# A planned attention block on one core: eleven seven-product steps instead of nine, their late halves issued behind the next step, and a causal mask added by a matmul

## The chip, the cores and the metric

The kernel runs on one NeuronCore of one Trainium2 chip. The metric is the device time of one execution in microseconds (us), lower is better. A core has a matmul engine (PE, with its weight loads shown as PEld), a vector engine (DVE), an activation engine (ACT), a general engine (POOL), a queue engine (SP) and 16 DMA engines that they share. Each engine works through its own instructions in the order in which they were written; an instruction that needs another engine's result waits on a semaphore, and everything behind it on its engine waits too.

## The reference

The input x is 256 rows of 4096 float32 numbers. With DEPTH = 1 only the attention layer and the two norms are computed, all to float32 accuracy:

```
proj = rms_norm(x, norm_attn) @ w_in        # 4096 x 16384
q, k, v, g = split(proj, 4)                 # 32 heads of 128 each
z = q @ k.T / sqrt(128)                     # strictly causal: s < t
log_fail = where(causal, log_sigmoid(-z), 0)
suffix = reverse_cumsum(log_fail) - log_fail
a = where(causal, exp(log_sigmoid(z) + suffix), 0)
o = a @ v
h = x + (o * silu(g)) @ w_out               # 4096 x 4096
out = rms_norm(h, final_norm)
```

## The kernel before

**Products.** The two large products, x by w_in and o by w_out, are cut into *units* of two pairs of columns and, inside a unit, into 16 *steps* of 256 rows of the weights. In one step a 2 x 2 block of activations meets a 2 x 2 block of weights. Written out plainly, this takes eight block products. A step listed in `SEVEN` uses a Strassen-like scheme of seven block products instead, for which three more sums of weight blocks have to be made. Every block product is done three times on PE (high x high, high x low, low x high), because each float32 number is split into a high part in the matmul's own reduced float32 format and the low rest. One such matmul is 128x512. The results of a unit gather in seven PSUM banks (`acc`); the DVE and ACT combine them at the unit's end (`combine`). Unit 0 of w_in and the first unit of w_out use eight products throughout ("plain"); units 1 to 15 of w_in and two units of w_out are "mixed".

**What a step needs.** SP loads two raw tiles (`raw..._0` and `raw..._1`, 256 KB in each of two DMAs) into a ring of 7 (`RAW_BUFS`). For a step with seven products POOL then adds a further block into the second tile by two accumulating DMAs (`add_block`). ACT casts a raw piece to the high part (`wh`), and DVE subtracts to get the low part (`wl`). A step with eight products has two such pieces of 128x1024. A step with seven has four, called parts 0 to 3: 128x1024, 128x512, 128x1024, 128x1024. Parts 2 and 3, the late half, are cast from sums: the DVE first makes three additions in place in the raw tiles (`sums`, L424), which wait for POOL's accumulation and for the low parts of parts 0 and 1. So a late part goes DVE sum, ACT cast, DVE subtraction, PE. The pieces of 128x1024 live in a ring of 5 pairs (`PAIRS`).

**Attention.** Each w_in unit of the mixed kind yields two heads. A head is turned by PE (`tr`), its scores are computed (`z`), ACT makes Abs, Exp, Ln and a scaling (`f`), DVE makes `f = max(z,0) + f`, and then a minimum with the constant `bound` zeroes what lies on and above the diagonal; a matmul by a triangle of -1 makes the suffix sums, ACT makes the weights `a`, and DVE masks `a` again by a minimum with `bound`; two matmuls give `o`. So DVE has two mask instructions of 128x256 per head.

**The order.** The text is not written in the order of the instructions. `Plan` (L95) keeps a clock of its own: every piece of work has an engine, an assumed cost and a due time (`key`); whenever an engine falls free in that plan, the ready work with the earliest due time is emitted on it. The products stand on PE in the order of the list `parts`; the due times of casts, subtractions and sums follow from it.

Of the kernel before, what the change touches and what calls it, by code (L numbers as in the profile page):

```python
# [19 lines left out]
P = 128  # L20
# [11 lines left out]
NS = KC // KT  # L32
EPS = 1e-6

WARM = 9

SEVEN = (1,3,5,7,8,10,11,13,14)
RAW_BUFS = 7
PAIRS = 5
SINGLES = 2
# [3 lines left out]
HEADS_AHEAD = 3  # L49
HEADS_LATER = 12  # L50
AHEAD, SUMS_AHEAD = 4.0, 3.0
PIPE = 0
BLOCKS_LATER = 2


# [175 lines left out]
def kernel(  # L231
# [10 lines left out]
    nc = Plan(tc)  # L242
# [22 lines left out]
    OUT0 = len(units)  # L265
# [7 lines left out]
    for u, (kind, w, cols) in enumerate(units):  # L273
        for s in range(NS):
            if kind == "single":
                if s % 2 == 0:
                    quads.append(((w, cols[0], s), (w, cols[0], s + 1)))
                b = ((1, 6), (7, 2))[u - LAST + 1]
                which = [plain_part(s % 2, *b)]
            else:  # L280
                quads.append(tuple((w, c, s) for c in cols))
                if kind == "plain":
                    which = [
                        plain_part(0, PLAIN["C11"], PLAIN["C21"]),
                        plain_part(1, PLAIN["C12"], PLAIN["C22"]),
                    ]
                else:
                    which = SEVEN_PARTS if s in (SEVEN) else EIGHT_PARTS
            for i, (k, place, prods) in enumerate(which):
                parts.append(  # L290
                    dict(u=u, s=s, i=i, tile=(len(quads) - 1, k), place=place, prods=prods, quad=len(quads) - 1,
                         seven=which is SEVEN_PARTS, size=place.stop - place.start)
                )

    if PIPE:
        late, turn = [], []
        for k, p in enumerate(parts):
            if p["seven"] and p["i"] > 1 and p["s"] < NS - 1:
                late.append(p)
                continue  # L300
            turn.append(p)
            if late and p["s"] != late[0]["s"] and (p["i"] == 1 if p["seven"] else p["i"] == 0):
                now = [q for q in late if q["s"] < p["s"] or q["u"] < p["u"]]
                turn += now
                late = [q for q in late if q not in now]
        assert not late and len(turn) == len(parts)
        parts = turn
# [43 lines left out]
    def ten(emit, *n):  # L351
        return nc.work("tensor", 90 + sum(tensor_ns(m) for m in n), emit, nc.here - 1e4, wait=400)

    def moved(engine, emit, sizes, key, after=None, hold=False, adds=False):
        issue = 550 if engine == "gpsimd" else 330
        return nc.work(
            engine, issue * len(sizes), emit, key, after=after, hold=hold, moves=[(4 * P * n, adds) for n in sizes]
        )
# [128 lines left out]
    forms = {}  # L487

    def new_forms(i, what):
        n = len(SEVEN_FORMS if i in SEVEN else EIGHT_FORMS)  # L490
# [11 lines left out]
    def sums_of(i, y, what, key):  # L502

        tt = nc.vector.tensor_tensor
        if i not in SEVEN:
# [83 lines left out]
    for _ in range(WARM):  # L589
# [2 lines left out]
    ident = ap.tile([P, P], F32, name="ident")  # L592
    make_identity(tc.nc, ident)

    bound = ap.tile([P, 1, P], F32, name="bound")
    nc.gpsimd.memset(bound, 3e38)
    nc.gpsimd.affine_select(
        out=bound, in_=bound, compare_op=ALU.is_gt, fill=0.0, base=0,
        pattern=[[0, 1], [1, P]], channel_multiplier=-1,
    )  # L600

    tri_f = ap.tile([P, P], F32, tag="qkl", name="tri_f")
# [184 lines left out]


    BW = 3 * P
    masked = bound.broadcast_to([P, 2, P])  # L790

    def diagonal(f):
        return f[:, 0 : 2 * P].rearrange("p (a b) -> p a b", a=2)

    def head(u, i):
        yield nc.take("att", "qkh")
        tr = att.tile([P, 2, S], F32, tag="att", name=f"tr{u}_{i}")
# [21 lines left out]
        yield ten(scores, *FULL_P, *FULL_S)  # L819
        nc.give("qkh")  # L820
        yield nc.take("f")

# [9 lines left out]
        yield dve(  # L832
            lambda: nc.vector.scalar_tensor_tensor(out=f, in0=z, scalar=0.0, in1=f, op0=ALU.max, op1=ALU.add), BW
        )
        yield dve(lambda: nc.vector.tensor_tensor(out=diagonal(f), in0=diagonal(f), in1=masked, op=ALU.min), 2 * P)
        yield nc.take("qkh", "qkl")
        fh = ap.tile([P, BW], F32R, tag="qkh", name=f"fh{u}_{i}")
        fl = ap.tile([P, BW], F32R, tag="qkl", name=f"fl{u}_{i}")
# [21 lines left out]
        yield act(weights_of, (BW, BW))  # L860
        nc.give("att")
        nc.start(gated_with(u, i))
        yield dve(lambda: nc.vector.tensor_tensor(out=diagonal(a), in0=diagonal(a), in1=masked, op=ALU.min), 2 * P)
        yield nc.until(("gated", u, i))
        o = st["both", u, i][:, 1, :]
        v = lambda t: st["gv", u][:, t, CW + i * P : CW + (i + 1) * P]
# [60 lines left out]
    def blocks_of_heads(s):  # L927
# [13 lines left out]
        if s in SEVEN:  # L941
# [217 lines left out]
    def products():  # L1159
        for g, (n, k) in enumerate(order):  # L1160
# [3 lines left out]
            if u < 1:  # L1164
                what = "s"
            elif u < OUT0:
                what = "n"
            elif u == OUT0:
                what = "o"
            else:  # L1170
                what = "r" if u > LAST - 2 and s in SEVEN else "p"
# [25 lines left out]
    for s in SEVEN:  # L1197
        nc.start(again(s))
    nc.start(single_h())
    nc.run()  # L1200
# [38 lines left out]
```

## Time and profile before

| | us |
|---|---|
| device time, median of 3 runs | 1755.45 (1755.28 to 1757.99) |
| profiled execution, first to last instruction (span) | 1754.0 |
| PE busy | 1736.9 (99%) |
| DVE busy | 1560.4 (89%) |
| ACT busy | 1166.4 (67%) |
| POOL busy | 295.7 (17%) |

The profile gives no time of the profiled execution beyond its span, so the span stands for it: 1.45 us under the median of the runs. Busy time counts an instruction to the end that the profile tells. On DVE the next instruction starts a little before that end when nothing holds it, so that an instruction of 1.22 us can have its successor 1.13 us after its start. The w_in units lie from the start to about 1400 us, the w_out units behind them.

### The profile page before, as it was taken

Reading aid. Unit: us, or ns where it says so; the run is one execution under the profiler, and the core shown is the slowest. Engines: PE = TensorE matmul, PEld = TensorE weight load, DVE = VectorE, ACT = ScalarE, POOL = GpSimd, SP = SyncE. Lnnn points to the kernel's source line nnn. Section 1 sums busy time; section 2 is a strip of 40 time slices with the busy share of each in tenths; the row PEclk is TensorE's granted clock in tenths of the full one; section 3 lists DMA queues with packets and bytes.
Section 4 is the critical chain, followed back from the end, with each engine's and each line's share of the span. In section 5 each row is a group of like instructions: output and inputs, shape, how many; then the busy total and the mean of one; then the engine's idle time right before and its main releaser. Section 6 shows DMA issues by size and latency. Waiting matters only on the chain.

```text
span 1754.0 us, 24699 instructions
## 1 busy us (share of the span) xinstructions
PE 1736.9 (99%) x7806; PEld 1427.1 (81%) x7806; DVE 1560.4 (89%) x1971; ACT 1166.4 (67%) x1594; POOL 295.7 (17%) x364
## 2 busy tenths in 40 slices
PE   8999999999999999999999999999999999999997
PEld 6888888888888888888888888888888888888885
DVE  7889999999999999999999999999999997899963
ACT  7975767676767676767676767676767675666543
POOL 0012121111111121211111111111112111111100
PEclk9999999999999999999999999999999999999998
DMA  9968777777777878787878787878786877889874
GB/s 340 316 192 224 230 218 229 223 223 226 222 228 217 239 210 239 208 245 210 240 208 245 208 239 206 242 202 245 200 246 200 262 244 239 229 245 271 257 236 156
DMA packets 242867, 405.86 MB, mean 231 GB/s; under 512 B 27520, under 2 KB 67968, under 8 KB 242736
## 3 DMA queue, kind: packets, MB, share of 16 engines
q1 hardware_dynamic: 193968, 352.15, 60.8%
q0 software_dynamic: 47184, 49.76, 17.3%
q10 hardware_dynamic: 1584, 2.38, 0.4%
q8 instruction: 61, 1.00, 0.2%
q14 instruction: 70, 0.57, 0.1%
HBM read 396.05 MB, written 8.13 MB: 230 GB/s over the span
## 4 chain that ended last, share of the span: by engine, by line
PE 92%; DVE 3%; issue 2%; DMA 2%; ACT 1%; SPq 0%; ACTq 0%; DVEq 0%
PE acc L115 87%; PE z L115 2%; DVE wl L115 2%; PE o L115 2%; DMA raw<-in_w_in_dram 1%; PE tr L115 1%; ACT wh L115 1%; DVE raw L115 0%; ACT h L115 0%; SPq L115 0%; DMA xres<-in_x_dram 0%; DMA raw<-in_w_out_dram 0%; ACTq L115 0%; DVE gv_sb L115 0%; DVE h L115 0%
## 5 line engine op out<-in xcount | busy, mean ns | idle before, releaser
L115 ACT CAST wh<-raw 128x1024 fp32r<-128x1024 f32 (+1 forms) x948 | 886.1, 976 | 476.1 <-issue 173.3
L115 DVE TENSOR_TENSOR wl<-raw,wh 128x1024 fp32r<-128x1024 f32 (+1 forms) x948 | 1032.1, 1131 | 125.3 <-ACT wh L115 118.6
L115 PE MATMUL acc<-wh,sh 128*128 128x512 f32 x1913 | 762.6, 399 | 2.4 <-DVE sh L115 2.1
L115 PE MATMUL acc<-wh,sl 128*128 128x512 f32 x1913 | 746.2, 390 | 0.0
L115 PE MATMUL acc<-wl,sh 128*128 128x512 f32 x1913 | 744.9, 389 | 0.8 <-DVE wl L115 0.8
L115 PEld LDWEIGHTS acc<-wh,sh 128*128 128x128 f32 x1913 | 359.4, 188 | 77.3 <-DVE gv_sb L115 3.9
L115 PEld LDWEIGHTS acc<-wh,sl 128*128 128x128 f32 x1913 | 359.1, 188 | 76.9 <-DVE sl L115 0.8
L115 PEld LDWEIGHTS acc<-wl,sh 128*128 128x128 f32 x1913 | 359.7, 188 | 71.5 <-DVE wl L115 1.5
L115 POOL DMA_DIRECT2D raw<-in_w_in_dram x270 | 236.1, 987 | 1075.7 <-DMA raw<-in_w_in_dram 403.1
L115 DVE TENSOR_TENSOR raw<-raw,raw 128x512 f32<-128x512 f32 x306 | 210.3, 687 | 5.1
L115 PE MATMUL acc<-wh,oh 128*128 128x512 f32 x494 | 193.2, 391 | 0.0
L115 PE MATMUL acc<-wl,oh 128*128 128x512 f32 x494 | 192.4, 389 | 0.6 <-DVE wl L115 0.6
L115 PE MATMUL acc<-wh,ol 128*128 128x512 f32 x494 | 192.3, 389 | 0.0
L115 PEld LDWEIGHTS acc<-wl,oh 128*128 128x128 f32 x494 | 92.8, 188 | 20.5 <-DVE wl L115 1.2
L115 PEld LDWEIGHTS acc<-wh,oh 128*128 128x128 f32 x494 | 92.8, 188 | 19.3 <-DVE gv_sb L115 0.4
L115 PEld LDWEIGHTS acc<-wh,ol 128*128 128x128 f32 x494 | 92.7, 188 | 19.2
L115 DVE TENSOR_TENSOR raw<-raw 128x512 f32<-128x512 f32 x153 | 104.5, 683 | 0.0
L115 POOL DMA_DIRECT2D raw<-in_w_out_dram x36 | 31.6, 992 | 132.5 <-DMA raw<-in_w_out_dram 66.2
L115 ACT ACTIVATE f<-f 128x384 f32<-128x384 f32 x96 | 50.5, 526 | 3.0
L115 DVE SCALAR_TENSOR_TENSOR f<-z,f 128x384 f32<-128x384 f32 x32 | 17.8, 557 | 31.2 <-ACT f L115 31.2
L115 POOL DMA_DIRECT2D p<-spill x33 | 20.3, 696 | 129.6 <-DVE ol L115 94.0
L115 ACT ACTIVATE gl<-gl 128x512 f32<-128x512 f32 x48 | 30.0, 625 | 7.3 <-DVE gl L115 7.3
(90 smaller groups left out, 745.9 us busy)
## 6 DMA issues: line engine op xcount, KB each, us to landing
raw<-in_w_in_dram SPq DMA_DIRECT2D x1020, 256.0 KB, 4.6
raw<-in_w_out_dram SPq DMA_DIRECT2D x256, 256.0 KB, 3.9
raw<-in_w_in_dram POOLq DMA_DIRECT2D x270, 128.0 KB, 5.2
raw<-in_w_out_dram POOLq DMA_DIRECT2D x36, 128.0 KB, 5.6
xr<-in_x_dram SPq DMA_DIRECT2D x16, 256.0 KB, 5.2
xres<-in_x_dram SPq DMA_DIRECT2D x16, 256.0 KB, 5.6
xs<-in_xT_dram SPq DMA_DIRECT2D x15, 256.0 KB, 5.3
spill<-gated POOLq DMA_DIRECT2D x15, 256.0 KB, 3.9
```

The lines of the kernel that those rows point to most:

```text
L115: return self.tc.keep_in_program_order(getattr(self.engine, name)(*args, **kw))
```

## The change

- In the mixed units of w_in the steps with seven products are now 1, 2, 4, 5, 7, 8, 9, 11, 12, 13, 14 (eleven; before 1, 3, 5, 7, 8, 10, 11, 13, 14, nine). The w_out units keep the old nine, under the name `SEVEN_OUT`. The forms of the activations follow the two lists.
- `PIPE = 1` switches on a block that was there but not used: in all mixed units the late half (parts 2 and 3) of a seven-product step up to step 13 is put behind parts 0 and 1 of the next step if that one is of seven, or behind its part 0 if it is of eight. Due times, the ring of pairs and the order on ACT, DVE, POOL and SP follow from the new list.
- The planner takes 950 instead of 550 ns for the issue of a POOL DMA.
- The mask: a constant `shut` of -1e30 on and above the diagonal, else 0, is multiplied by an identity, both in bfloat16, and added to the scores in PSUM by one more 128x256 matmul per head. Both DVE mask instructions of a head are gone.

```diff
-SEVEN = (1,3,5,7,8,10,11,13,14)
+SEVEN = (1, 2, 4, 5, 7, 8, 9, 11, 12, 13, 14)
+SEVEN_OUT = (1, 3, 5, 7, 8, 10, 11, 13, 14)
...
-PIPE = 0
+PIPE = 1
+LATE_UNTIL = 14
...
-                    which = SEVEN_PARTS if s in (SEVEN) else EIGHT_PARTS
+                    which = SEVEN_PARTS if s in (SEVEN if u < OUT0 else SEVEN_OUT) else EIGHT_PARTS
...
     if PIPE:
         late, turn = [], []
         for k, p in enumerate(parts):
-            if p["seven"] and p["i"] > 1 and p["s"] < NS - 1:
+            if p["seven"] and p["i"] > 1 and p["s"] < LATE_UNTIL:
                 late.append(p)
                 continue
             turn.append(p)
...
-        issue = 550 if engine == "gpsimd" else 330
+        issue = 950 if engine == "gpsimd" else 330
...
+    ident_h = ap.tile([P, P], BF16, name="ident_h")
+    nc.gpsimd.tensor_copy(ident_h, ident)
+    shut = ap.tile([P, 2, P], BF16, name="shut")
+    nc.gpsimd.memset(shut, SHUT)
...
+            nc.tensor.matmul(z[:, 0 : 2 * P], ident_h, shut.rearrange("p a b -> p (a b)"), start=False, **kw)
...
-        yield dve(lambda: nc.vector.tensor_tensor(out=diagonal(f), in0=diagonal(f), in1=masked, op=ALU.min), 2 * P)
...
-        yield dve(lambda: nc.vector.tensor_tensor(out=diagonal(a), in0=diagonal(a), in1=masked, op=ALU.min), 2 * P)
```

The DVE's order at steps 7 and 8 of the w_in unit 10, before (`raw167` and `raw168` are their tiles, both steps of seven products in both kernels; `wl...<-raw...` is a subtraction, `raw...<-raw...` a sum):

```order
L115 TENSOR_TENSOR raw167_0_8483<-raw167_0_8483,raw167_1_8453 128x2x256
L115 TENSOR_TENSOR raw167_1_8453<-raw167_0_8483,raw167_1_8453 128x2x256
L115 TENSOR_TENSOR a9_1_8632<-a9_1_8632,bound_111 128x256
L115 TENSOR_TENSOR raw167_0_8483<-raw167_0_8483 128x2x256
L115 TENSOR_TENSOR wl504_8622<-raw167_1_8453,wh504_8621 128x1024
L115 TENSOR_TENSOR wl505_8642<-raw167_0_8483,wh505_8641 128x1024
L115 TENSOR_TENSOR wl506_8669<-raw168_0_8550,wh506_8668 128x1024
L115 TENSOR_TENSOR gated9_8506<-o9_1_8644,gated9_8506 128x256
L115 TENSOR_TENSOR raw168_0_8550<-raw168_0_8550,raw168_1_8494 128x2x256
L115 TENSOR_TENSOR raw168_1_8494<-raw168_0_8550,raw168_1_8494 128x2x256
L115 TENSOR_TENSOR raw168_0_8550<-raw168_0_8550 128x2x256
L115 TENSOR_TENSOR wl508_8695<-raw168_1_8494,wh508_8694 128x1024
```

The same two steps on DVE in the changed kernel:

```order
L118 TENSOR_TENSOR raw167_0_8721<-raw167_0_8721,raw167_1_8633 128x2x256
L118 TENSOR_TENSOR gated9_8652<-o9_1_8802,gated9_8652 128x256
L118 TENSOR_TENSOR wl542_8824<-raw168_0_8757,wh542_8823 128x1024
L118 TENSOR_TENSOR raw167_1_8633<-raw167_0_8721,raw167_1_8633 128x2x256
L118 TENSOR_TENSOR raw168_0_8757<-raw168_0_8757,raw168_1_8732 128x2x256
L118 TENSOR_TENSOR raw167_0_8721<-raw167_0_8721 128x2x256
L118 TENSOR_TENSOR raw168_1_8732<-raw168_0_8757,raw168_1_8732 128x2x256
L118 TENSOR_TENSOR wl544_8841<-raw167_1_8633,wh544_8840 128x1024
L118 TENSOR_TENSOR wl545_8852<-raw167_0_8721,wh545_8851 128x1024
```

The sums of one step now stand between those of the other: between the sum that writes `raw167_1` and the subtraction that needs its cast there is one more 128x512 sum before, and three now; and the mask instruction of `a` is gone.

The second place is the start of a head on DVE, before: `gv_sb9` is the last combining of unit 9's banks, `f9_0` the first head's instruction behind ACT's Abs, Exp, Ln and scaling.

```order
L115 SCALAR_TENSOR_TENSOR gv_sb9_8207<-acc9_3_7545,rin_v_1046,gv_sb9_8207 128x512
L115 TENSOR_TENSOR wl486_8278<-raw161_1_8141,wh486_8277 128x1024
L115 TENSOR_TENSOR wl487_8300<-raw161_0_8193,wh487_8299 128x1024
L115 TENSOR_TENSOR wl488_8330<-raw162_0_8208,wh488_8329 128x1024
L115 SCALAR_TENSOR_TENSOR f9_0_8345<-z9_0_8331,f9_0_8345 128x384
L115 TENSOR_TENSOR f9_0_8345<-f9_0_8345,bound_111 128x256
```

The same place on DVE in the changed kernel:

```order
L118 SCALAR_TENSOR_TENSOR gv_sb9_8349<-acc9_3_7702,rin_v_1064,gv_sb9_8349 128x512
L118 TENSOR_TENSOR raw161_0_8369<-raw161_0_8369,raw161_1_8341 128x2x256
L118 TENSOR_TENSOR raw161_1_8341<-raw161_0_8369,raw161_1_8341 128x2x256
L118 TENSOR_TENSOR raw161_0_8369<-raw161_0_8369 128x2x256
L118 SCALAR_TENSOR_TENSOR f9_0_8505<-z9_0_8492,f9_0_8505 128x384
L118 TENSOR_TENSOR raw162_0_8401<-raw162_0_8401,raw162_1_8383 128x2x256
```

Between the last combining and `f9_0` stood three subtractions of 128x1024, and now stand three sums of 128x512; the mask behind `f9_0` is gone.

More of the change, by code (lines that the diff above doesn't have):

```diff
@@ L35 @@
 WARM = 9
-SEVEN = (1,3,5,7,8,10,11,13,14)
+SHUT = -1e30
+SEVEN = (1, 2, 4, 5, 7, 8, 9, 11, 12, 13, 14)
+SEVEN_OUT = (1, 3, 5, 7, 8, 10, 11, 13, 14)
 RAW_BUFS = 7
@@ L489, in new_forms @@
     def new_forms(i, what):
-        n = len(SEVEN_FORMS if i in SEVEN else EIGHT_FORMS)
+        n = len(SEVEN_FORMS if i in (SEVEN if what == "s" else SEVEN_OUT) else EIGHT_FORMS)
         h = sp.tile([P, n, P], F32R, tag=f"xh{i}", name=f"{what}h{i}")
@@ L504, in sums_of @@
         tt = nc.vector.tensor_tensor
-        if i not in SEVEN:
+        if i not in (SEVEN_OUT if what == "p" else SEVEN):
             y4 = y.rearrange("p (a b) c -> p a b c", a=KT)
@@ L593 @@
     make_identity(tc.nc, ident)
-    bound = ap.tile([P, 1, P], F32, name="bound")
-    nc.gpsimd.memset(bound, 3e38)
+    ident_h = ap.tile([P, P], BF16, name="ident_h")
+    nc.gpsimd.tensor_copy(ident_h, ident)
+    shut = ap.tile([P, 2, P], BF16, name="shut")
+    nc.gpsimd.memset(shut, SHUT)
     nc.gpsimd.affine_select(
-        out=bound, in_=bound, compare_op=ALU.is_gt, fill=0.0, base=0,
-        pattern=[[0, 1], [1, P]], channel_multiplier=-1,
+        out=shut, in_=shut, compare_op=ALU.is_ge, fill=0.0, base=0,
+        pattern=[[0, 2], [-1, P]], channel_multiplier=1,
     )
@@ L789 @@
     BW = 3 * P
-    masked = bound.broadcast_to([P, 2, P])
-    def diagonal(f):
-        return f[:, 0 : 2 * P].rearrange("p (a b) -> p a b", a=2)
     def head(u, i):
@@ L817, in scores @@
             nc.tensor.matmul(z[:, P:BW], qk[:, 1, 0:P], qk[:, 0, :], start=False, **kw)
-        yield ten(scores, *FULL_P, *FULL_S)
+            nc.tensor.matmul(z[:, 0 : 2 * P], ident_h, shut.rearrange("p a b -> p (a b)"), start=False, **kw)
+        yield ten(scores, *FULL_P, *FULL_S, 2 * P)
         nc.give("qkh")
@@ L940, in blocks_of_heads @@
         nc.give("gh")
-        if s in SEVEN:
+        if s in SEVEN_OUT:
             key = min(place_at(OUT0, s + 1), place_of[OUT0 + 1, s] - 3e3)
@@ L1170, in products @@
             else:
-                what = "r" if u > LAST - 2 and s in SEVEN else "p"
+                what = "r" if u > LAST - 2 and s in SEVEN_OUT else "p"
             if starts[u, b] == (n, k):
@@ L1196 @@
         nc.start(blocks_out(U + k + 1, c))
-    for s in SEVEN:
+    for s in SEVEN_OUT:
         nc.start(again(s))
```

## The prediction, made before the changed kernel had run

> **What bounds the kernel now.** I read the page's totals and slices first, to see which engine is full.
>
> ```profile
> PE 1736.9 (99%) x7806; PEld 1427.1 (81%) x7806; DVE 1560.4 (89%) x1971; ACT 1166.4 (67%) x1594; POOL 295.7 (17%) x364
> ...
> PE   8999999999999999999999999999999999999997
> ...
> DVE  7889999999999999999999999999999997899963
> ...
> PEclk9999999999999999999999999999999999999998
> ```
>
> PE is busy from end to end at full clock; DVE stands at nine tenths in every slice of the w_in stage. A busy PE could still be one that is held up inside, so I read the waits of PE over the whole span, then a stretch of ten mixed units (it runs from one `gl` instruction to the tenth after it, one per unit) and a stretch of nothing but products.
>
> ```profile
> PE acc L115 <- DVE sh L115: 2.1, 2, 1.1
> PE acc L115 <- DVE wl L115: 1.4, 2, 0.8
> ```
>
> ```profile
> 195.20 0.69 DVE L115 SCALAR_TENSOR_TENSOR gl<-gv_sb,gl 128x512 f32<-128x512 f32 x1
> ...
> 1063.86 0.69 DVE L115 SCALAR_TENSOR_TENSOR gl<-gv_sb,gl 128x512 f32<-128x512 f32 x1
> ```
>
> ```profile
> 195.20:1063.80 868.60, 868.58 (x3932) 714.51 (x3931) 799.74 (x961) 586.33 (x770) 163.07 (x190) 1.00 0.78 224
> 1500.00:1550.00 50.00, 50.00 (x222) 41.39 (x221) 47.63 (x57) 30.54 (x40) 8.74 (x10) 1.00 0.87 245
> ```
>
> The columns are PE, PEld, DVE, ACT, POOL. A mixed unit lasts (1063.86 - 195.20) / 10 = 86.87 us, and PE never waits in it: PE is the bound. DVE is busy 799.74 / 10 = 79.97 us of a unit and idle 6.9. A matmul of 128x512 takes 50.00 / 222 = 0.225 us of PE (the means of 0.39 us that the groups show overlap), so a block product of three takes 0.676 us.
>
> The question is what DVE's 6.9 idle us are, because the change adds DVE work. Its waits in the ten units, and three places of its timeline:
>
> ```profile
> DVE wl L115 <- ACT wh L115: 40.9, 82, 0.6
> DVE f L115 <- ACT f L115: 21.0, 20, 1.3
> DVE wl L115 <- DMA raw<-in_w_in_dram: 1.8, 4, 0.4
> ```
>
> ```profile
> 509.76 0.69 DVE L115 TENSOR_TENSOR raw<-raw,raw 128x512 f32<-128x512 f32 x1
> 510.36 0.68 DVE L115 TENSOR_TENSOR wl<-raw,wh 128x512 fp32r<-128x512 f32 x1
> 510.97 0.69 DVE L115 TENSOR_TENSOR raw<-raw,raw 128x512 f32<-128x512 f32 x1
> ...
> 516.42 1.42 DVE L115 TENSOR_TENSOR raw<-raw,raw 128x512 f32<-128x512 f32 x2
> 517.75 0.68 DVE L115 TENSOR_TENSOR raw<-raw 128x512 f32<-128x512 f32 x1
> 519.07 6.37 DVE L115 TENSOR_TENSOR wl<-raw,wh 128x1024 fp32r<-128x1024 f32 x6 [0.63 <-ACT wh L115]
> ...
> 525.96 1.21 DVE L115 TENSOR_TENSOR wl<-raw,wh 128x1024 fp32r<-128x1024 f32 x1
> 527.09 0.68 DVE L115 TENSOR_TENSOR gv_sb<-acc,gv_sb 128x512 f32<-128x512 f32 x1
> ...
> 533.87 0.74 DVE L115 SCALAR_TENSOR_TENSOR gv_sb<-acc,rin_v,gv_sb 128x512 f32<-128x512 f32 x1
> 534.53 3.48 DVE L115 TENSOR_TENSOR wl<-raw,wh 128x1024 fp32r<-128x1024 f32 x3
> 538.81 0.56 DVE L115 SCALAR_TENSOR_TENSOR f<-z,f 128x384 f32<-128x384 f32 x1 [0.80 <-ACT f L115]
> 539.40 0.42 DVE L115 TENSOR_TENSOR f<-f,bound 128x256 f32<-128x256 f32 x1
> ...
> 551.22 0.42 DVE L115 TENSOR_TENSOR a<-a,bound 128x256 f32<-128x256 f32 x1
> 551.56 1.82 DVE L115 TENSOR_TENSOR wl<-raw,wh 128x1024 fp32r<-128x1024 f32 x2
> ```
>
> Start to start, DVE spends 0.60 us on a 128x512 instruction (509.76, 510.36, 510.97), 1.13 on a 128x1024 one (525.96 to 527.09) and 0.34 on a mask (551.22 to 551.56). The gap at 519.07 is the common one, 8.2 times a unit: the last three sums of a step are made, and the subtraction of the late part waits for ACT to cast what the second sum wrote. So 4.1 of the 6.9 idle us come from the order itself, 2.1 from the wait for ACT's chain in the two heads, 0.2 from loads. DVE is not far ahead of PE with nothing to do; it trips over its own order.
>
> **The change, part by part.** *Products.* Two steps per unit go from eight products to seven: 2 x 0.676 = 1.35 us less PE per unit, 15 x 1.35 = 20.3 us in all. As PE never waits, all of it is on the path, as long as the others follow.
>
> *The mask matmul.* The trace has no 128x256 matmul of bfloat16. Bounds from the nearest row: half of a 128x512 slot if the width decides, 0.113 us, and a whole slot, 0.225, so 3.6 to 7.2 us for 32 of them. I take 0.113, since these matmuls follow one another by width in the same pipeline. The Trainium skill, "TensorE: Matmul & The Clock Gate", section on the warm matmul gap, gives N / 2.4 GHz + 2.5 ns start to start, which as an estimate is 109 ns here and 3.5 us in all; for 512 columns it gives 215.7 ns, where this trace has 225. PE's own floor is then 86.87 - 1.35 + 0.23 = 85.75 us a unit, and 20.3 - 3.6 = 16.7 us less over the kernel.
>
> *DVE work.* A step that goes from eight to seven gains one 128x1024 subtraction, one 128x512 subtraction and three sums: 1.13 + 4 x 0.60 = 3.54 us, two steps 7.1 us a unit. The masks take away 4 x 0.34 = 1.36. So 79.97 + 7.1 - 1.36 = 85.7 us: against PE's 85.75 there is nothing left for DVE to wait in. That is the core of this case.
>
> *DVE order.* What is late next, once the late halves move? By the order shown, the subtraction of a late part stands behind one 128x512 sum before, and behind at least two DVE instructions now: counted over all late parts, 90 of 306 had only 0.6 us of DVE work between the sum and the subtraction, and 2 of 366 have now; 26 have 1.2 us. The chain sum, cast, subtraction took 519.07 - 517.75 = 1.32 us from the end of the sum, so 1.2 leaves about 0.1. The 4.1 us of waiting become some 0.3. With each wait that goes, the tail that busy time counts before it (1.21 - 1.13 = 0.08) goes too, 8 x 0.08 = 0.65. Two dependent sums in a row cost 517.75 - 516.42 = 1.33 us and not 1.20, and f with its mask (538.81 to 539.40) 0.59; both become rarer, estimated 0.5 a unit. DVE's pure work is then 85.7 - 0.65 - 0.5 = 84.5 us.
>
> *The wait for f stays.* ACT's timeline at the same head:
>
> ```profile
> 535.14 0.63 ACT L115 ACTIVATE gl<-gv_sb 128x512 f32<-128x512 f32 x1
> 535.68 1.04 ACT L115 CAST wh<-raw 128x1024 fp32r<-128x1024 f32 x1
> 536.62 0.49 ACT L115 ACTIVATE f<-z 128x384 f32<-128x384 f32 x1
> 537.14 1.64 ACT L115 ACTIVATE f<-f 128x384 f32<-128x384 f32 x3
> ```
>
> `gl` waits for the last `gv_sb` (done 533.87 + 0.74 = 534.61), and the chain of f ends at 538.78. In the changed order ACT has no cast between `gl` and `f`, so the chain could end at 534.61 + 0.54 + 2.16 = 537.3; but DVE has three sums there instead of three subtractions and is back at 534.53 + 3 x 0.605 = 536.35. It waits 1.0 us at the first head of each unit (0.80 here). For the second head the mean of the waits row, 21.0 / 20 = 1.05, is the one end and nothing the other; I take 0.3, because DVE has more ready work now. With 0.2 for loads: waits of 0.3 + 1.3 + 0.2 = 1.8 us.
>
> *Sum.* DVE needs 84.5 + 1.8 = 86.3 us a unit, PE 85.75: DVE becomes the bound by half a us, and a unit goes from 86.87 to 86.3. Over 15 units this is -0.57 x 15 = -8.5 us; the profiled execution would go from 1754.0 to 1745.5, and the median, 1.45 above it, to 1747.
>
> *What lies beside it.* ACT gains 1.05 + 0.6 us of casts per step, 3.3 a unit on 58.6 of 86.9; it stays covered, but DVE waits for it at any late cast. SP issues as many loads as before. POOL issues four more DMAs a unit:
>
> ```profile
> SPq L115 <- DVE wl L115: 976.2, 527, 8.7
> ```
>
> ```profile
> raw<-in_w_in_dram SPq DMA_DIRECT2D x1020, 256.0 KB, 4.6
> ...
> raw<-in_w_in_dram POOLq DMA_DIRECT2D x270, 128.0 KB, 5.2
> ```
>
> ```profile
> L115 POOL DMA_DIRECT2D raw<-in_w_in_dram x270: 852/866/1241, 77.5 to 1373.6; - x135
> ```
>
> 4 x 0.87 = 3.5 us more on an engine that is busy 16.3 of 86.9; behind them in its queue stand only the spills of `gated`, for which nobody waits before w_out. The waits of SP show that a load starts when DVE's subtraction frees a raw tile, so tiles held longer start loads later: see the second rival. In the w_out units the products stay as many, PE is full there (50.00 of 50.00) and cannot gain from a better DVE order. The two extra sets of activation forms fall into unit 0, where DVE is at seven and eight tenths. All that costs nothing while DVE stays within its 86 us.
>
> **The rivals.** *DVE keeps up completely.* If the second head waits for nothing and the small bubbles are fewer than I take, DVE needs less than 85.75 and PE stays the bound: -16.7 us, 1739. For it: PE has up to five pairs of work in hand, 6.8 us where they are two products each, which rides out a late wait. Against it: 85.7 of 85.75 before any saving.
>
> *Loads come late and DVE is the bound (slower).* A seven-step's two raw tiles are now held through the next step's first parts, while the ring has seven. Counted along DVE's order, from the release of a slot to the first sum that needs POOL's addition in its new tile, the least DVE work is 15.0 us before, and 10.5 and 10.6 now, at steps 8 and 5. Load, POOL's second issue and landing need 4.6 + 0.87 + 5.2 = 10.7 by their medians, with DMAs at 78% busy and some 3% more to carry. If these two sums wait 1 us each, a unit is 88.3 us and the kernel 1754 + 1.4 x 15 = 1775, so 1777 in the median. It decides from the point where DVE's waits pass 86.87 - 84.5 = 2.4 us a unit; I have 1.8. The far end, all of today's 6.9 idle us kept on 85.7, would be 92.6 a unit and +86 us; the order shown excludes most of it.
>
> *Nothing to see.* Waits of 2.2 to 2.6 us a unit leave the time within 0.2% (3.5 us), which is about what a measurement of this kernel can tell from no change.
>
> *PE slows down because it is made to wait.* The clock falls where PE idles at the end:
>
> ```profile
> 1700.00:1750.00 50.00, 42.28 (x187) 34.69 (x185) 24.64 (x42) 21.65 (x35) 0.00 (x0) 0.95 0.48 157
> 1750.00:1754.00 4.00, 0.00 (x0) 0.00 (x0) 0.00 (x0) 0.00 (x0) 0.00 (x0) 0.50 0.64 238
> ```
>
> If each unit had one PE pause long enough to halve the clock for some 3.4 us, 1.7 us a unit would be lost, +26 us on top of the pause. The longest PE wait on products is 1.1 us and the clock stays 1.00 around it, so I give it little. The page named above says in its part on the clock gate that the half rate comes after an idle window of about 3.4 us; the row of 0.50 agrees.
>
> **How the numbers follow.** DVE just about full, a gain of 3.5 to 14 us: 0.38. PE's floor reached, 1737 to 1741: 0.17. Within 0.2%: 0.16. Slower by late loads or DVE waits beyond 2.4 us: 0.26. Slower with a lower clock: 0.03. So faster 0.55, same 0.16, slower 0.29. The likeliest case gives 1747, its own range is 1741 to 1752. The range for 8 in 10 goes from the floor, 1738, up to most of the slow rival, 1773.
>
> **What would show it.** In the changed profile: DVE busy at 97% or more of the stretch of w_in, and its wait for ACT's `wh` down from 4.1 to below 1 us a unit; the wait for `f` still near 1 us at the first head; products fewer by 90 matmuls; PE waiting for `wl` a little in each unit, where it now waits in none. If PE shows no waits there, the first rival holds. If DVE or ACT wait for DMAs or for POOL's additions at steps 5 and 8, the second does. I am wrong in kind if the waits for `wh` remain as they were, or if the w_out units become longer.

## The result, and the profile after

The changed kernel takes 1781.43 us (median of 4 runs, 1780.61 to 1782.3) against 1755.72 us for the kernel before, measured beside it: 1.0141 times as long, 95% interval 1.0129 to 1.0153. It is slower by 25.7 us, where 8.5 us less were predicted. The profiled execution has a span of 1780.6 us (before 1754.0).

The page of the changed kernel, its totals, slices and the chain that ended last:

```profile
PE 1735.4 (97%) x7748; PEld 1407.2 (79%) x7748; DVE 1630.3 (92%) x2065; ACT 1221.1 (69%) x1656; POOL 343.7 (19%) x425
...
PE   9999999999999999999999999999999999999997
...
DVE  7889999989999999899999998999998997898963
...
PEclk9999999999999999999999999999999999999999
...
PE 37%; DVE 26%; DMA 18%; issue 11%; ACT 6%; POOL 0%; SPq 0%; DVEq 0%; ACTq 0%; POOLq 0%
```

PE does 58 recorded matmuls fewer and is hardly less busy; DVE has 70 us more. The last row is the news. In the chain of before, shown next, PE had 92%, DVE 3% and DMA 2%; now PE has little more than a third, and DMA stands at 18%.

```profile
PE 92%; DVE 3%; issue 2%; DMA 2%; ACT 1%; SPq 0%; ACTq 0%; DVEq 0%
```

Ten mixed units of the changed kernel, from the fourth `gl` on DVE to the fourteenth: the two rows that bound them, and the stretch (PE, PEld, DVE, ACT, POOL, clock, DMA share, GB/s). Below it stands the same stretch of the kernel before.

```profile
366.47 0.68 DVE L118 SCALAR_TENSOR_TENSOR gl<-gv_sb,gl 128x512 f32<-128x512 f32 x1
...
1253.59 0.69 DVE L118 SCALAR_TENSOR_TENSOR gl<-gv_sb,gl 128x512 f32<-128x512 f32 x1
```

```profile
366.45:1253.55 887.10, 866.85 (x3891) 700.88 (x3890) 845.64 (x1021) 620.09 (x811) 195.14 (x230) 1.00 0.81 226
```

```profile
368.85:1237.90 869.05, 868.75 (x3932) 714.51 (x3931) 799.89 (x961) 586.32 (x770) 163.10 (x190) 1.00 0.79 224
```

A unit lasts (1253.59 - 366.47) / 10 = 88.71 us; before it was 86.90 between the same two rows. PE, which had next to no idle time in its units (0.3 us in ten), now has (887.10 - 866.85) / 10 = 2.0 us of it in each. From the first `gl` to the last the kernel takes 25.1 us more (1333.1 against 1308.0), from there to the end 3.0 more, and up to the first 1.5 less: 26.6 together, which is the difference of the spans.

The waits of DVE in these ten units (us in all, times, longest):

```profile
DVE raw L118 <- DMA raw<-in_w_in_dram: 22.8, 20, 2.4
DVE f L118 <- ACT f L118: 11.3, 20, 0.8
DVE wl L118 <- ACT wh L118: 3.8, 10, 0.4
DVE raw L118 <- DVE wl L118: 0.8, 1, 0.8
DVE qk_sb L118 <- ACT qk_sb L118: 0.6, 1, 0.6
```

And those of PE:

```profile
PE tr L118 <- DVE qk_sb L118: 7.0, 10, 1.3
PE o L118 <- ACT gated L118: 4.8, 13, 0.6
PE z L118 <- DVE fl L118: 3.6, 5, 0.9
PE acc L118 <- DVE wl L118: 3.4, 5, 1.0
```

`wl` waits for `wh` 0.4 us a unit where it waited 4.2 between the same rows before (4.1 in the ten units of the prediction). The late halves were to bring that about; the run with them alone shows below that they do not do it by themselves. In its place stands a wait that the kernel before did not have: `raw <- DMA raw`, a sum that waits for POOL's accumulating DMAs, 2.3 us a unit. All but about 1 of the 22.8 us stands at steps 5 and 8, the rest at step 12. PE in turn waits for DVE and ACT in the heads, and a little for `wl`.

One unit shows where. DVE's timeline of the changed kernel from 543 us:

```profile
543.48 1.22 DVE L118 TENSOR_TENSOR wl<-raw,wh 128x1024 fp32r<-128x1024 f32 x1
...
554.64 0.68 DVE L118 TENSOR_TENSOR raw<-raw,raw 128x512 f32<-128x512 f32 x1
556.78 1.90 DVE L118 TENSOR_TENSOR raw<-raw,raw 128x512 f32<-128x512 f32 x3 [1.46 <-DMA raw<-in_w_in_dram]
...
562.46 0.56 DVE L118 SCALAR_TENSOR_TENSOR f<-z,f 128x384 f32<-128x384 f32 x1 [0.31 <-ACT f L118]
563.40 1.23 DVE L118 TENSOR_TENSOR wl<-raw,wh 128x1024 fp32r<-128x1024 f32 x1 [0.38 <-ACT wh L118]
...
574.74 0.69 DVE L118 TENSOR_TENSOR raw<-raw,raw 128x512 f32<-128x512 f32 x1 [1.19 <-DMA raw<-in_w_in_dram]
```

The queues behind the first of these waits, SP's and then POOL's:

```profile
544.73 0.80 SPq L118 DMA_DIRECT2D raw<-in_w_in_dram  x2
```

```profile
549.10 1.75 POOL L118 DMA_DIRECT2D raw<-in_w_in_dram  x2 [11.96 <-DVE wl L118]
```

The wait at 556.78 is that of step 5, the one at 574.74 that of step 8. At step 5 the subtraction that ends at 543.48 + 1.22 = 544.70 frees a raw tile; SP issues the load into it, in two halves, from 544.73 on; the halves land at 548.54 and 549.10. POOL issues one addition for each half, at 549.10 and 549.63, about half a us behind each landing; the second lands at 556.65, and the sum starts at 556.78. POOL's row names a DVE subtraction as what it waited for. One did end at 548.64, but the first half landed within 0.1 us of that, so the row cannot tell the two apart; the second addition needs the second half in any case. The chain has little slack in it: only an earlier release or a shorter transfer could bring this sum forward, or else DVE must have other work to do until then. It takes 12.1 us, in which DVE has 12.1 - 1.46 = 10.6 us of work. In the median of the ten units it takes 11.4 us at step 5 and 12.7 at step 8.

### The profile page after: what moved, and what is told of

It is laid out like the page before. It is cut to its first block, busy times and chain, and to the rows that moved or that the text cites. A ratio compares the mean times of both kernels' runs of the same rounds, so it can differ in the third digit from the quotient of the medians.

```text
span 1780.6 us, 24894 instructions
## 1 busy us (share of the span) xinstructions
PE 1735.4 (97%) x7748; PEld 1407.2 (79%) x7748; DVE 1630.3 (92%) x2065; ACT 1221.1 (69%) x1656; POOL 343.7 (19%) x425
## 4 chain that ended last, share of the span: by engine, by line
PE 37%; DVE 26%; DMA 18%; issue 11%; ACT 6%; POOL 0%; SPq 0%; DVEq 0%; ACTq 0%; POOLq 0%
PE acc L118 36%; DMA raw<-in_w_in_dram 16%; DVE wl L118 15%; DVE raw L118 8%; ACT wh L118 2%; DVE gv_sb L118 2%; ACT f L118 2%; DMA raw<-in_w_out_dram 1%; DMA xres<-in_x_dram 1%; ACT gl L118 1%; PE o L118 1%; POOL raw L118 0%; DVE qk_sb L118 0%; SPq L118 0%; DVE gl L118 0%
## 5 line engine op out<-in xcount | busy, mean ns | idle before, releaser
L118 ACT CAST wh<-raw 128x1024 fp32r<-128x1024 f32 (+1 forms) x1008 | 940.4, 969 | 419.7 <-PE acc L118 165.6
L118 DVE TENSOR_TENSOR wl<-raw,wh 128x1024 fp32r<-128x1024 f32 (+1 forms) x1008 | 1090.5, 1119 | 52.5 <-ACT wh L118 50.4
L118 PE MATMUL acc<-wh,sh 128*128 128x512 f32 x1883 | 746.4, 396 | 1.6 <-DVE sh L118 1.0
L118 PE MATMUL acc<-wl,sh 128*128 128x512 f32 x1883 | 736.3, 391 | 5.9 <-DVE wl L118 4.6
L118 PE MATMUL acc<-wh,sl 128*128 128x512 f32 x1883 | 734.8, 390 | 0.0
L118 POOL DMA_DIRECT2D raw<-in_w_in_dram x330 | 284.4, 965 | 1094.8 <-DVE wl L118 460.7
L118 DVE TENSOR_TENSOR raw<-raw,raw 128x512 f32<-128x512 f32 x366 | 247.1, 686 | 35.8 <-DMA raw<-in_w_in_dram 31.1
L118 DVE TENSOR_TENSOR raw<-raw 128x512 f32<-128x512 f32 x183 | 124.0, 684 | 0.0
L118 ACT COPY qkT<-tr 128x512 f32<-128x512 f32 x32 | 18.6, 580 | 46.9 <-PE tr L118 46.9
L118 PEld LDWEIGHTS o<-a,gv_sb 128*128 128x128 f32 x128 | 22.3, 189 | 18.2 <-ACT gated L118 15.9
```

What stands on the lines that cost most here:

```text
L118: return self.tc.keep_in_program_order(getattr(self.engine, name)(*args, **kw))
```

## The experiments

The theory after the result is that DVE bounds the mixed units and that the sums at steps 5 and 8 make it wait for POOL's additions (A). Against it stands that the changed order has another limit, DVE's added work itself or PE's waits in the heads, beside which the additions only look like the cause (B). Diffs are against the changed kernel; once the mask edit has been shown, only its first line is repeated. "Per unit" always means the same ten units, from the fourth `gl` to the fourteenth.

**Without the additions at steps 5 and 8.** In the w_in units the sums of these two steps start from the tile as it was loaded: the block that POOL would add is left out, so something else is computed there. DVE's work is the same, and so is the order: on DVE, ACT and PE the two traces have the same instructions on the same tiles (buffer numbers aside), place by place.

```diff
-                nc.start(add_block(q))
+                if parts[quad_parts[q][0]]["u"] < OUT0 and quads[q][0][2] in (5, 8):
+                    nc.start(no_block(q))
+                else:
+                    nc.start(add_block(q))
...
+    def no_block(q):
+        yield nc.until(("raw", q, 1))
+        nc.tell(("T3", q))
```

> The changed kernel, but at steps 5 and 8 of the w_in units POOL's two accumulating DMAs are left out (the sums are made from the raw tile as it was loaded, so two of eleven steps per unit compute something else). Theory A (late additions: DVE waits at exactly these two steps for POOL's accumulation because the ring of raw tiles is held longer): a unit of 88.6 us loses the 2.1 us of these waits, 86.5 us, so about 1781 - 2.1 x 14 = 1752, within 5 us. Theory B (DVE is simply full and any wait moves to another place): 1775 to 1781.

It took 1753.78 us, 0.9988 of before (0.9975 to 1.0002): 27.7 us less than the changed kernel. A unit lasts 86.4 us in the profiled execution, which at 1749.91 us is the fastest of ten runs (the slowest took 1759.82). DVE's waits in ten units of it:

```profile
DVE f L118 <- ACT f L118: 11.3, 20, 0.8
DVE wl L118 <- ACT wh L118: 3.8, 10, 0.4
DVE qk_sb L118 <- ACT qk_sb L118: 1.9, 5, 0.7
DVE raw L118 <- DMA raw<-in_w_in_dram: 0.4, 1, 0.4
```

The waits for `f` and `wh` are those of the changed kernel to a tenth; only the wait for the additions is gone, 2.2 us a unit, and 2.3 of the 88.7 us with it. So A holds: with every order the same, the unit loses just these waits. Of B it leaves that DVE's added work and its other waits keep the unit at 86.4, above the 85.75 that PE was reckoned to need. The kernel also moves less by POOL's DMAs, so it does not tell a late addition from crowded DMAs; the next run leaves all of them in.

**A planner that reckons with longer transfers.** Nothing is left out. The planner only takes a transfer to begin 1900 ns behind its issue instead of 1300, and so writes the sums later in DVE's order.

```diff
-            begin = max(self.now + cost * (k + 1) / len(moves) + 1300, self.moved)
+            begin = max(self.now + cost * (k + 1) / len(moves) + 1900, self.moved)
```

> The changed kernel with one number of the planner raised: a transfer is taken to need 1900 instead of 1300 ns before it begins. The instructions stay the same, the order shifts. By the order the least DVE work between the release of a raw tile and the first sum rises from 10.5 to 11.9 us, and the first use of a plain load from 6.2 to 7.3. Theory A (the order is planned with transfers that are shorter than the chip's, so DVE waits at steps 5 and 8): the waits of 2.4 us a unit fall below 0.5, so 1781 - 2 x 15 = 1751, within 5 us. If the additions were late because the DMA engines or POOL are full, the order would not help: 1775 or more.

1742.41 us (1741.06 to 1744.74), 0.9919 of before (0.9904 to 0.9934): faster than expected, and faster than both kernels. Waits in ten units, DVE's three and PE's only one:

```profile
DVE f L118 <- ACT f L118: 8.2, 9, 0.9
DVE wl L118 <- ACT wh L118: 5.4, 22, 0.4
DVE raw L118 <- DMA raw<-in_w_in_dram: 1.9, 3, 1.1
```

```profile
PE acc L118 <- DVE wl L118: 0.6, 1, 0.6
```

The same instructions and the same DMAs need 85.9 us a unit in another order. So the changed kernel lost its gain to its order, not to the work that was added. Not all of it is the later place of the sums, though. At step 5 the pair of additions takes as long as in the changed kernel (7.4 us in the median from POOL's first issue to the second landing, 7.6 there) and lands before its sum is due. At step 8 the pair itself got shorter, 5.9 us against 7.9, though all DMAs are there. Late sums and crowded transfers are thus not fully parted: the order sets both.

**Further the same way: 2500 ns.**

```diff
-            begin = max(self.now + cost * (k + 1) / len(moves) + 1300, self.moved)
+            begin = max(self.now + cost * (k + 1) / len(moves) + 2500, self.moved)
```

> The planner's latency at 2500 instead of 1900 ns. By the order the first sum of step 8 has 11.3 us from the release of its tile (11.9 at 1900, 10.5 at 1300), the others 12.7 and more. Theory A: some waits at step 8 alone, 1742 to 1755. If 1900 were a lucky hit and not a cause: about 1770 or more.

A miss: 1776.22 us, 1.0112 (1.0097 to 1.0127). By what was written down beforehand, this makes 1900 a lucky hit. The additions are in time, and another wait has come. DVE's waits in ten units, and a head in its timeline:

```profile
DVE f L118 <- ACT f L118: 25.2, 20, 1.6
DVE wl L118 <- ACT wh L118: 10.6, 20, 0.7
DVE raw L118 <- DMA raw<-in_w_in_dram: 1.6, 1, 1.6
```

```profile
540.53 0.74 DVE L118 SCALAR_TENSOR_TENSOR gv_sb<-acc,rin_v,gv_sb 128x512 f32<-128x512 f32 x1
541.19 0.68 DVE L118 TENSOR_TENSOR raw<-raw,raw 128x512 f32<-128x512 f32 x1
541.79 0.68 DVE L118 TENSOR_TENSOR raw<-raw 128x512 f32<-128x512 f32 x1
544.02 0.56 DVE L118 SCALAR_TENSOR_TENSOR f<-z,f 128x384 f32<-128x384 f32 x1 [1.55 <-ACT f L118]
```

Here the combining and the sums behind it are over before ACT's chain has ended. DVE waits for `f` at all 20 heads of the ten units, 1.3 us in the mean. A unit lasts 88.4 us, nearly that of the changed kernel with quite another wait. The planner's number is therefore no model of the transfer that one could make "right"; it shuffles the order, and each order has its own waits.

**POOL's issue back to 550 ns**, the small part of the change.

```diff
-        issue = 950 if engine == "gpsimd" else 330
+        issue = 550 if engine == "gpsimd" else 330
```

> The changed kernel with the planner's old 550 ns for a POOL issue. The order has the same least 10.5 and 10.6 us at steps 8 and 5, so theory A: 1776 to 1786, the 950 did neither harm nor good. If it was the new cost that upset the order: below 1765.

1789.10 us, 1.0183 (1.0162 to 1.0205), 3 us above what was expected and 8 above the changed kernel. The additions keep DVE waiting as before the edit (23.0 us in ten units, 22.8 in the changed kernel), so the larger number did nothing against this wait. It is no better model of the issue either: the profile shows 0.86 us for one, but the second of a pair starts 0.61 us behind the first in the median.

**The mask on DVE again.** Both minimum instructions return and the mask matmul goes; the rest stays.

```diff
-            nc.tensor.matmul(z[:, 0 : 2 * P], ident_h, shut.rearrange("p a b -> p (a b)"), start=False, **kw)
...
+        yield dve(lambda: nc.vector.tensor_tensor(out=diagonal(f), in0=diagonal(f), in1=masked, op=ALU.min), 2 * P)
...
+        yield dve(lambda: nc.vector.tensor_tensor(out=diagonal(a), in0=diagonal(a), in1=masked, op=ALU.min), 2 * P)
```

> The changed kernel with the masks on DVE as before, without the mask matmul. Theory A (DVE bound in a loop with the raw tiles): DVE work rises by 1.36 us a unit, of which the waits for additions at steps 5 and 8 take up a part (by the order their shortage falls from 2.9 to 1.3 us), so +0 to +10 us on 1781. Theory B (DVE full, waits independent): +1.36 x 16 = +22 us, 1803. If PE still set the time: -3.6 us.

A miss in sign: 1760.28 us, 1.0022 (1.0012 to 1.0031), 21 us faster than the changed kernel though DVE has 4 x 0.34 = 1.36 us more to do in each unit. The waits for additions went down to a third:

```profile
DVE raw L118 <- DMA raw<-in_w_in_dram: 7.3, 7, 2.0
DVE wl L118 <- ACT wh L118: 6.4, 10, 1.0
DVE f L118 <- ACT f L118: 2.6, 8, 0.4
```

Two things changed at once here, DVE's work and the planner's reckoning, so the next run parts them.

**The mask matmul, planned as if DVE still did the masks.** The planner spends DVE time on two instructions that are not emitted, and does not count the extra matmul.

```diff
-        yield ten(scores, *FULL_P, *FULL_S, 2 * P)
+        yield ten(scores, *FULL_P, *FULL_S)
...
+        yield dve(lambda: None, 2 * P)
...
+        yield dve(lambda: None, 2 * P)
```

> The changed kernel with the mask matmul, but the planner still reckons with the two mask instructions on DVE (nothing is emitted for them), so that the order is close to that of the run with the masks on DVE, which took 1760. Theory A (it is the order that made the change of the mask cost 21 us): 1755 to 1768, although DVE has 22 us less to do. If the matmul itself, or the chain through it, costs the time: about 1780.

1753.73 us, 0.9981 (0.997 to 0.9991). It issues exactly the instructions of the changed kernel and is 27.7 us faster. Apart from the masks and the mask matmul, DVE, ACT and PE have the very order of the run before it, so these two runs give the price of the masks in one order: the mask matmul is innocent, and moving the masks to PE is worth some 7 us (1.0022 against 0.9981 of before). What its presence did to the order cost about four times as much. DVE still waits 1.0 us a unit for additions here, nearly all at step 5:

```profile
DVE raw L118 <- DMA raw<-in_w_in_dram: 10.4, 10, 2.4
```

**The mask matmul alone, in the kernel before.**

```diff
-SEVEN = (1, 2, 4, 5, 7, 8, 9, 11, 12, 13, 14)
+SEVEN = (1, 3, 5, 7, 8, 10, 11, 13, 14)
...
-PIPE = 1
+PIPE = 0
...
-        issue = 950 if engine == "gpsimd" else 330
+        issue = 550 if engine == "gpsimd" else 330
```

> The kernel before with the mask matmul alone: nine steps, no late halves. Both theories: PE is the bound, so the 32 matmuls add 3.6 us if half a slot each, 7.2 if a whole one, and DVE's 22 us less work bring nothing: 1759 to 1763. If DVE's waits had held the time before: below 1755.

1759.02 us, 1.0017 (1.0007 to 1.0027): 2.6 us slower than before. Where PE is the bound, what DVE saves brings nothing. The 32 matmuls cost 0.08 us each with the interval from 0.04 to 0.15, if all of it is theirs: the order moved a little too.

**The late halves alone, in the kernel before** (nine steps, masks on DVE, 550 ns).

```diff
-SEVEN = (1, 2, 4, 5, 7, 8, 9, 11, 12, 13, 14)
+SEVEN = (1, 3, 5, 7, 8, 10, 11, 13, 14)
...
-            nc.tensor.matmul(z[:, 0 : 2 * P], ident_h, shut.rearrange("p a b -> p (a b)"), start=False, **kw)
...
-        issue = 950 if engine == "gpsimd" else 330
+        issue = 550 if engine == "gpsimd" else 330
```

> The kernel before with the late halves moved alone: nine steps, masks on DVE. Theory A: PE has 86.87 us a unit, DVE 77.7 and some 4 of waits, so PE stays the bound: 1753 to 1758, and the waits for casts behind sums fall from 4.1 to about 1 us a unit. If holding raw tiles longer is harmful by itself: above 1762.

1753.45 us, 0.9982 (0.9972 to 0.9991). A unit lasts 86.3 us instead of 86.9 although the products are those of before; of the 6.8 us that the w_in units win, the part behind the last `gl` gives back 6.4 (349.8 against 343.4). The wait for `wh` fell less than expected: it is 3.3 us a unit in all, and the part behind sums went from 3.5 to 1.8, where about 1 was expected. The stretch of ten units shows PE full, as it was before; the waits of the weight loads in before may be what is won. First PE's stretch and DVE's wait in this kernel, then the weight loads' waits in the ten units of the kernel before:

```profile
365.95:1228.95 863.00, 863.00 (x3931) 716.86 (x3930) 803.27 (x961) 604.18 (x771) 163.26 (x190) 1.00 0.79 226
```

```profile
DVE wl L118 <- ACT wh L118: 33.4, 83, 0.9
```

```profile
PEld z L115 <- ACT qkT L115: 4.2, 10, 0.4
PEld tr L115 <- DVE gated L115: 3.7, 10, 0.5
PEld acc L115 <- DVE gv_sb L115: 2.9, 10, 0.4
```

Each of these came once a unit, and none is left in this kernel. PE counted as busy through all of them.

**The eleven steps alone** (masks on DVE, no late halves, 550 ns).

```diff
-PIPE = 1
+PIPE = 0
...
-            nc.tensor.matmul(z[:, 0 : 2 * P], ident_h, shut.rearrange("p a b -> p (a b)"), start=False, **kw)
...
-        issue = 950 if engine == "gpsimd" else 330
+        issue = 550 if engine == "gpsimd" else 330
```

> Eleven seven-product steps alone: masks on DVE, late halves in their own step, the planner's old 550 ns. DVE needs 84.7 + 0.9 + 2.9 us behind sums + 0.3 to 2.3 for f = 88.8 to 90.8 us a unit, so 1783 to 1813. If DVE were not the bound of the eleven steps: 1735 to 1755.

1774.77 us, 1.0103 (1.0088 to 1.0119), less than expected. DVE does not wait for additions or `f` in the ten units, but 1.6 us a unit for `wh` on top of its full work, and PE waits 15.0 us for `wl` in the ten units. Why `f` is never late here was not found. Fewer products, slower kernel: the eleven steps need something that keeps DVE going.

**Eleven steps and the mask matmul, without late halves.**

```diff
-PIPE = 1
+PIPE = 0
```

> Eleven seven-product steps and the mask matmul, but the late halves stay in their own step. Theory A: the waits for POOL's additions go (the shortest DVE work from the release of a raw tile to the first sum rises from 10.5 to 13.3 us), but the waits of subtractions for ACT's casts come back, about 2.8 us a unit by the order: DVE needs 83.4 + 0.9 + 2.8 + 1.3 to 2.3 = 88.4 to 89.4 us a unit, so 1775 to 1795. If the late halves alone made the kernel slow: 1739 to 1755.

1777.17 us, 1.0117 (1.0101 to 1.0132). No wait for additions; `wl` waits for `wh` 2.4 us a unit instead, and PE for `wl` 1.3. Late halves trade the one wait for the other, and in the order that was written they are worth nothing: 1777.17 against 1781.43.

**Ten steps** (1, 3, 5, 7, 8, 10 to 14), late halves, masks on DVE: less work for DVE than eleven.

```diff
-SEVEN = (1, 2, 4, 5, 7, 8, 9, 11, 12, 13, 14)
+SEVEN = (1, 3, 5, 7, 8, 10, 11, 12, 13, 14)
...
-            nc.tensor.matmul(z[:, 0 : 2 * P], ident_h, shut.rearrange("p a b -> p (a b)"), start=False, **kw)
```

> Ten seven-product steps (1, 3, 5, 7, 8, 10, 11, 12, 13, 14), late halves moved, masks on DVE. Theory A: DVE needs 81.2 us a unit, 4 to 5 with its waits, so 85 to 86.2; PE's floor is 86.87 - 0.68 = 86.2, so PE is the bound and one product less per unit is gained: -0.68 x 15 = -10, 1746, if loads do not stop it (no sum has less than 12.7 us, but one first part of step 11 has 4.6 us from the release of its tile): 1743 to 1756. If late halves as such make DVE wait: above 1760.

A miss: 1768.97 us, 1.007 (1.0055 to 1.0085). The waits of PE in ten units, and one of them in its timeline beside DVE's:

```profile
PE acc L118 <- DVE qk_sb L118: 13.5, 10, 1.9
```

```profile
535.26 0.50 PE L118 MATMUL acc<-wh,sh 128*128 128x512 f32 x1 [1.17 <-DVE qk_sb L118]
```

```profile
533.33 1.22 DVE L118 TENSOR_TENSOR wl<-raw,wh 128x1024 fp32r<-128x1024 f32 x1
534.47 0.74 DVE L118 SCALAR_TENSOR_TENSOR qk_sb<-acc,rin_v,qk_sb 128x512 f32<-128x512 f32 x1
```

PE stops once a unit for a PSUM bank that DVE frees by the last `qk_sb`, which stands behind a subtraction of 1.22 us here. That the five seven-steps in a row brought it there is likely, not shown. And DVE waits 2.6 us a unit for `f`. Less work on the fullest engine did not help, since a new place to wait came with it.

**The faster order with the masks on DVE** (the 1900 ns of above and the mask edit together).

```diff
-            begin = max(self.now + cost * (k + 1) / len(moves) + 1300, self.moved)
+            begin = max(self.now + cost * (k + 1) / len(moves) + 1900, self.moved)
...
-            nc.tensor.matmul(z[:, 0 : 2 * P], ident_h, shut.rearrange("p a b -> p (a b)"), start=False, **kw)
```

> The kernel of the planner's latency of 1900 ns (1742), with the masks on DVE instead of the matmul. If DVE, and not the loads, sets the time once the order is right, the 1.34 us of masks a unit show nearly in full: 84.7 + 2 = 86.7 us a unit against 85.9, 1742 + 0.8 x 15 = 1754. If PE sets it, the matmul's 3.6 us go and the time is 1738 to 1742.

1749.15 us, 0.9958 (0.9943 to 0.9973), between the two expectations and 6.7 us above the 1900 ns kernel, or 0.67 us a unit where DVE works 1.36 more. The planner reckoned anew here, and the order differs in many places, so this is the price of masks and order together. The pair above, with one order, has the masks at 0.5 us a unit (87.3 against 86.8), so less than half of DVE's added work lengthened that unit.

All kernels side by side; unit and waits are those of the ten units of the profiled execution, in us a unit:

| kernel | time, us | unit | DVE waits for additions | for `f` | for `wh` |
|---|---|---|---|---|---|
| before | 1755.72 | 86.9 | 0 | 2.1 | 4.2 |
| changed | 1781.43 | 88.7 | 2.3 | 1.1 | 0.4 |
| no additions at 5 and 8 | 1753.78 | 86.4 | 0 | 1.1 | 0.4 |
| 1900 ns | 1742.41 | 85.9 | 0.2 | 0.8 | 0.5 |
| 2500 ns | 1776.22 | 88.4 | 0.2 | 2.5 | 1.1 |
| POOL 550 ns | 1789.10 | 89.0 | 2.3 | 1.1 | 0.5 |
| masks on DVE | 1760.28 | 87.3 | 0.7 | 0.3 | 0.6 |
| mask matmul, order of masks | 1753.73 | 86.8 | 1.0 | 0.4 | 1.0 |
| mask matmul alone | 1759.02 | 87.0 | 0 | 2.2 | 5.6 |
| late halves alone | 1753.45 | 86.3 | 0 | 1.5 | 3.3 |
| eleven steps alone | 1774.77 | 87.9 | 0 | 0 | 1.6 |
| eleven steps and mask matmul | 1777.17 | 88.0 | 0 | 0.6 | 2.4 |
| ten steps, masks on DVE | 1768.97 | 87.7 | 0 | 2.6 | 1.7 |
| 1900 ns, masks on DVE | 1749.15 | 86.6 | 0.2 | 0.4 | 0.2 |

## Why the prediction was wrong

The sum was 84.5 us of DVE work and 1.8 us of waits, 86.3 a unit. Measured are 88.71, of which 39.3 / 10 = 3.9 are the waits of the view above; the rest, 84.8, is the work with its small gaps. So the work was right to 0.3 us, and the failure lies in the waits, term by term:

- *Waits of `wl` behind the sums, 0.3:* right in size by luck. The view has 0.38, but all of it is one wait a unit for a cast that stands behind `f` on ACT (563.40 in the timeline); behind the sums nothing is left.
- *The wait for `f`, 1.3:* right, 1.13 measured; at most 0.8 at a head where I had 1.0 for the first, and 0.31 at the second (562.46) where I took 0.3.
- *Loads, 0.2:* **this is the step that failed.** It measured 2.3, and the 2.1 us too little in this one term are most of the 2.4 by which the unit is longer than forecast. The run without the additions at steps 5 and 8 shows the rest of the sum to hold: in its fastest run the unit is 86.4, where 86.3 was forecast. The second rival named the two steps, the mechanism and the point from which it decides; I had put it at 0.26.

Inside that rival the DVE work between release and sum was 10.5 and 10.6 us, and the timeline has 10.6. What came out too short was the transfer, 10.7 us by medians against 12.1 (and 12.6 at step 8 of the same unit, from the release at 562.15 to 574.74). The load was as assumed, 549.10 - 544.73 = 4.4 us. The addition was 0.87 + 5.2 = 6.1 in my sum and 556.65 - 549.10 = 7.6 here: the second issue came earlier than I had it, 0.5 us behind the first, and its transfer took 7.0 us instead of 5.2. That was no odd unit. I had taken the median over all steps, and the pair of additions takes quite different times at different steps, alike from unit to unit: in the medians of the ten units 7.6 us at step 5 and 7.9 at step 8, but 4.2 at step 7. The kernel before already had 7.6 and 7.0 at its steps 7 and 8, with time to spare. Over all steps the pair takes 6.9 us in the median and 8.1 at the upper tenth; before 6.2 and 7.5. Even by medians the margin was -0.1 us, which means a wait at every such step, and I costed it at nothing in the forecast.

The other steps:

- *PE's floor of 85.75:* about right. The 1900 ns kernel needs 85.9 with PE hardly waiting (0.6 us in ten units), so the floor lies no higher.
- *"PE never waits in it: PE is the bound":* only nearly. The late halves alone brought 0.6 us a unit with the same products, and the weight loads' short waits, which the busy time of PE hides, went away with it. That the one is due to the other is likely from their places, not shown.
- *"4.1 of the 6.9 idle us come from the order itself":* too much. Of the waits for `wh` in the ten units of before, 60 of 84 stand behind sums, 3.5 us a unit. With the late halves alone DVE still waits 3.3 us a unit for `wh`. PE is full there (863.00 of 863.00 us), so DVE must wait somewhere; that new waits only took the place of the old is argued, not shown.
- *The mask matmul, 3.6 us:* 2.6 where it was added alone, and 3.6 lies within that run's interval.
- *"The masks take away 4 x 0.34 = 1.36":* true as work, and yet the kernel with the masks back was faster. I read the order that the planner had made, counted the tightest places in it, and still priced the parts of the change as if the order were independent of them.
- *A lower PE clock:* did not come. PE's waits here are up to 1.6 us long and the clock stays at 1.00. The Trainium skill, "TensorE: Matmul & The Clock Gate", in its part on the clock gate, has the half rate only after an idle window of about 3.4 us; this trace agrees.
- *DVE busy at 97% or more of the stretch:* it was busy 845.64 of 887.10 us, 95%, since it waits more than forecast.
- *The w_out units costing nothing:* not right. From the last `gl` to the end the changed kernel takes 3.0 us more; the prediction had named this as a sign of being wrong in kind. The kernels tried here vary from 343.3 to 350.9 us in this part, and I could not tie that to one of their differences; it stays open.

Also open: whether one more raw tile in the ring would do what the later sums did. It wasn't tried.

## What to carry to other kernels

When an engine is planned to within 1% of its capacity, the forecast hangs on the latest of the transfers that it needs: compare the time from the release of a buffer to its first use with the transfer's time at that very step of a trace, or, where the order is new, with the upper tenth of the transfers' times, not with a median over all steps. In a kernel whose order comes from a planner, an edit is priced by the order that it makes: here the same instructions took 1742, 1754, 1776, 1781 and 1789 us, so try a few of the planner's constants on the chip before judging the edit. And read the waits after each try, since removing one wait often lets another one decide.

## What the runs showed of the hardware that was not expected

How long POOL's accumulating DMAs took differed more with their place in the order than with the busy share of the DMAs. In the ten units of the changed kernel a pair takes 4.2 us at step 7 and 7.9 at step 8. At step 8 of the 1900 ns kernel it takes 5.9, though the DMAs' busy share over the ten units is higher there, 0.84 against 0.81. The longer times go with more loads from SP: between 5 us before POOL's first issue and 4 us behind it SP issues 10 at steps 5 and 8, and 3 at step 7 (means of the ten units). That these loads are the cause was not tested by itself. Single ones, from the list of DMA issues of the changed kernel, and all of them from the view of the raw tiles on POOL (shortest, median, longest):

```profile
raw<-in_w_in_dram POOLq DMA_DIRECT2D x330, 128.0 KB, 5.6
```

```profile
DMA to landing us min/median/max: 2.9/5.6/9.4
```

The Trainium skill, "DMA: Bandwidth & Descriptors", section on the anatomy of one DMA on the SWDGE path, gives 2.0 us + bytes / 436e3, which as an estimate is 2.3 us for 128 KB; the shortest of these took 2.9 and the median 5.6, among other traffic and with an accumulation. And a PE shown as busy almost without a gap (868.75 of 869.05 us in ten units of before) still had 0.6 us a unit to give: with the late halves alone the same products took 86.3 us a unit.
